# RWKV scan in an RWKV / DeltaNet / Mamba trunk: the chunk inverse applied to the scan's operands in batches, ahead of the scan

## The chip, the cores and the metric

The kernel runs on one core of a Trainium2 chip. The metric is the device time of one execution in microseconds; the time shown of the kernel before is the median of three executions. One more execution was profiled, and all rows below come from that one.

## What is computed

One residual layer over 16 learned meta tokens and 1024 frames of width 1024: a normalised input goes through one wide projection, then through three groups of heads (gated DeltaNet, RWKV-7, Mamba-2), and their outputs through one output projection. The change touches RWKV-7 alone: 8 heads of 64, each with a 64x64 state that is updated frame by frame.

```python
def rwkv7_recurrence(r, w, k, v, a, b):
    """S_t = S_{t-1} diag(w_t) + (S_{t-1} a_t) b_t^T + v_t k_t^T,  y_t = S_t r_t."""
    def step(state, inp):
        r_t, w_t, k_t, v_t, a_t, b_t = inp
        sa = jnp.einsum("bhvk,bhk->bhv", state, a_t)
        state = (state * w_t[:, :, None, :] + sa[..., None] * b_t[:, :, None, :]
                 + v_t[..., None] * k_t[:, :, None, :])
        return state, jnp.einsum("bhvk,bhk->bhv", state, r_t)
    ...
# in rwkv7_group: a = -kk, b = kk * a, with kk the l2-normalised keys
```

## The kernel before, in words

The kernel is a list of units: six of DeltaNet (`unit_a`, one head of 128 each), four of RWKV (`unit_b`, two heads of 64 each), two of Mamba (`unit_c`), and at the end the output stage (`unit_o`). Each unit is a Python generator. Its first part is projections: `proj` multiplies a 128-column weight tile with all frames, in pieces of some 350 columns, eight steps of the contraction and three float32r products a step; these are the matmuls `pj`. They are dense work of TensorE (PE) that waits for little. Its second part is the unit's own algebra, many short steps on PE, ScalarE (ACT) and VectorE (DVE), each of which hands over with a `yield`.

`schedule` (L1193) decides the order. It keeps an estimate of PE's clock, takes a unit's next short step when it believes its inputs to be ready, and fills PE with single projection matmuls until then. The units' order is the constant `PLAN`; some projections are put into a queue by `later` and are due at a given time. What the generators issue is then placed on each engine by the tile framework's scheduler, so the order of instructions on an engine is fixed before the run, and PE executes its list in order. `Meter` (L97) records every operation of the short steps, so most rows have the line L97 and are told apart by the tiles' names.

Short steps take their PSUM tiles through `ps` (L119): a unit has a lane, and a lane has two PSUM tiles in turn (`GB`), so a third one waits until the first has been read.

`unit_b` (L641) works on 17 chunks of 64 frames, the first one mostly padding. For each chunk it builds, for two heads at a time on the two halves of the 128 partitions: `ar` (the decayed a and r), `bk` (the decayed b and k), their masked products `gms` from the matmuls `bgr` (L97), and `bt`, the transposes of `bk` (matmuls `bbT`, ACT copies `bbt`). The lower triangular system of a chunk is inverted ahead of the scan, in blocks of 32: diagonal blocks by `solve32` on DVE, the block below by the 32x32 matmuls `bm1`, `bm2` (L796 to L806). The inverse stands in `gms[0]`, called `gb` in the scan; `gk` is the product with the keys, `v1_` the values.

The scan (L813 to L861) goes through the chunks one by one, three steps a chunk with a `yield` between them. Step one fills the PSUM tile `bsi`: `gk·v + ar·st`, and the output's first two terms beside it; ACT copies the first half to `b_x` (L830). Step two multiplies `b_x` by the inverse into the PSUM tile `bu` (L832) and starts the state update with `b_k·v`; DVE scales by `ib` into `u_`, a part of the tile `buv`. Step three adds `b_k·u`, makes the new state `sn` (tile `b_s`) on DVE, and adds `gb·u` to the output in `bsi`, which ACT copies to `by` (L852). Every one of these products is two matmuls of 64x64, one for each half of the array (`both`).

Of the kernel before, what the change touches and what calls it, by code (L numbers as in the profile page):

```python
# [19 lines left out]
MUL, ADD, SUB, MAX = ALU.mult, ALU.add, ALU.subtract, ALU.max  # L20
# [43 lines left out]
def bc(ap, axis, n):  # L64

    ap = ap.unsqueeze(axis)
    shape = list(ap.shape)
    shape[axis] = n
    return ap.broadcast_to(tuple(shape))
# [32 lines left out]
class Trunk:  # L102
# [538 lines left out]
    def unit_b(self, p):  # L641
        nc, sm = self.nc, self.sm
        v, act, pe, pool, sync = self.engines
        ident = self.ident
        yield 1, "proj"
        k, r = (self.one([128, 17, 64], f"b{x}{p}") for x in "kr")
# [4 lines left out]
        at_c = lambda t, c: t[c // 9][:, c % 9]  # L651
# [14 lines left out]
        for i, (out, bias) in enumerate(((e1[:, :, 1:], self.w0), (at, self.a0))):  # L666
            for s, e in ((0, 8), (8, 16), (16, 17)):
                ps = self.ps(f"bw{p}_{i}{s}")
# [5 lines left out]
        for s in range(0, 17, 3):  # L674
            e = min(s + 3, 17)
# [10 lines left out]
        ar, bk = ([self.one([128, 9 - i, 128], f"b{x}{p}_{i}") for i in range(2)] for x in ("ar", "bk"))  # L686

        ib = sm.tile([128, 17], F32, tag="b_ib", name="b_ib")
        hs = (slice(0, 64), slice(64, 128))
# [3 lines left out]
        ps = self.ps(f"bn{p}")  # L693
# [21 lines left out]
        gms = [[self.one([128, 9 - i, 128], f"bgm{p}_{x}{i}") for i in range(2)] for x in range(2)]  # L715
        banks = ((1, 5), (5, 9), (9, 13), (13, 17), (0, 1))
        for s, e in banks:
            pair = [self.ps(f"bgr{p}_{x}{s}") for x in range(2)]
            for c in range(s, e):
                for x in range(2):  # L720
                    for h in range(2):
                        pe.matmul(pair[x][hs[h], 128 * (c - s): 128 * (c - s) + 128], at_c(bk, c)[hs[h], hs[x]], at_c(ar, c)[hs[h]],
                                  start=True, stop=True)
# [9 lines left out]
        for s, e in banks:  # L733
            ps = self.ps(f"bbT{p}_{s}")
# [29 lines left out]
        uv = [self.one([128, 9 - i, 128], f"buv{p}_{i}") for i in range(2)]  # L764
        for s, e in ((0, 1), (1, 9), (9, 17)):
            ps = self.ps(f"bvT{p}_{s}")
            n, m = (e - s + 1) // 2, min(e - s, 2)
            for j in range(n):
                pe.transpose(ps[: 64 * m, 128 * j: 128 * j + 128], v_[:, 64 * (s + 2 * j): 64 * (s + 2 * j + m)], ident)
            for j in range(m):  # L770
                for h in range(2):
                    x = s % 9 + j
# [4 lines left out]
        for w in range(2):  # L777
            ps = self.ps(f"bbon{p}{w}")
# [14 lines left out]
        for i, (c0, c1) in enumerate(split):  # L793
            n = c1 - c0
# [15 lines left out]
        yield 12  # L810


        yt = self.one([128, 8, 128], f"by{p}")  # L813
        st, to_a, to_r = None, hs[0], hs[1]
        for c in range(17):
            gb, gk, a_r, b_k, uvc = (at_c(t, c) for t in (gms[0], gms[1], ar, bt, uv))
            u_, v1_ = uvc[:, 0:64], uvc[:, 64:]

            def both(out, cols, lhs, part, rhs, start, stop):
                for h in range(2):  # L820
                    pe.matmul(out[hs[h], cols], lhs[hs[h], part], rhs[hs[h]], start=start, stop=stop, skip_group_check=True)

            pq = self.ps(f"bsi{p}_{c}")
            both(pq, hs[0], gk, to_a, v1_, True, c == 0)
            if c:
                both(pq, hs[0], a_r, to_a, st, False, True)
                both(pq, hs[1], gk, to_r, v1_, True, False)
                both(pq, hs[1], a_r, to_r, st, False, False)
            x = self.tmp("b_x")
            act.copy(x[:, 0:64], pq[:, 0:64])  # L830
            yield
            pu = self.ps(f"bu{p}_{c}")  # L832
            both(pu, hs[0], gb, to_a, x[:, 0:64], True, True)
            if c < 16:
                pd = pu[:, 64:128]
                both(pu, hs[1], b_k, hs[1], v1_, True, False)
            v.tensor_scalar(u_, pu[:, 0:64], ib[:, c: c + 1], None, MUL)
            yield
            if c < 16:
                both(pu, hs[1], b_k, hs[0], u_, False, True)  # L840
                sn = self.tmp("b_s")
                w_ = wc[:, c + 1: c + 2]
                if c:
                    nc.scalar.activation(sn[:, 64:128], st, AF.Copy, scale=w_)
                    v.scalar_tensor_tensor(sn[:, 0:64], pd, w_, sn[:, 64:128], MUL, ADD)
                else:
                    v.tensor_scalar(sn[:, 0:64], pd, w_, None, MUL)
                sn = sn[:, 0:64]
            if c:
                both(pq, hs[1], gb, to_r, u_, False, True)  # L850
                for h in range(2):
                    nc.scalar.copy(yt[hs[(c - 1) % 2], (c - 1) // 2, hs[h]], pq[hs[h], 64:128])  # L852
                self.lag = max(0.2, self.lag - 0.21)
            if c < 16:
                st = sn
            if c == GATE:
                yield 8
                g = self.one([128, 17, 64], f"bg{p}")
                gated = self.later(36 + p, self.shifted(36 + p, 12 + p, g, gate=True), DUES[4])
                g = flat(g)  # L860
            else:  # L861
                yield
# [16 lines left out]
        for w in range(2):  # L879
            ps = self.ps(f"byT{p}_{w}")  # L880
# [518 lines left out]
```

## Time and profile before

| | |
|---|---|
| Median of three executions | 1450.17 us (1448.45 to 1453.15) |
| The profiled execution's own time | 1442.35 us |
| Span from its first to its last instruction | 1440.4 us |
| Mean granted TensorE clock | 0.985 |
| Instructions | 28351 |
| PE / weight loads / DVE / ACT / GpSimd (POOL) busy | 96% / 83% / 65% / 50% / 12% |

How to read it: a matmul's record begins when it enters the array; matmuls are pipelined and their ends are modelled, so a duration is longer than the time a matmul adds to a row of them. That time is the distance from one start to the next. A float32 matmul leaves two records and two weight loads, a float32r one and a transpose leave one of each. The size written before a shape, such as 64\*64 or 128\*128, is the part of the array that the matmul uses.

### The profile page before, as it was taken

What the parts mean: (1) busy time and instruction counts of PE and PEld (TensorE: products, weight loads), DVE (VectorE), ACT (ScalarE), POOL (GpSimd) and SP (SyncE); (2) the same over time, 40 slices, a digit from 0 to 9 for tenths busy, and PEclk for the clock granted to TensorE, in tenths of its full rate; (3) what the DMA queues carried; (4) which work ended last, traced back from release to release, by engine and by line L of the source; (5) the groups of instructions that cost most, each with busy time, mean ns of one, the idle gap of its engine ahead of it and who ended that gap; (6) DMA issues with size and microseconds to landing.
All of it is one profiled execution on the core that took longest, in us unless ns stands there. A gap on an engine that the chain in (4) does not pass through costs nothing.

```text
span 1440.4 us, 28351 instructions
## 1 busy us (share of the span) xinstructions
PE 1389.7 (96%) x10801; PEld 1188.8 (83%) x10801; DVE 935.4 (65%) x2610; ACT 719.9 (50%) x2020; POOL 172.4 (12%) x223
## 2 busy tenths in 40 slices
PE   4999999999999999999999999999999999899997
PEld 4999888778788789979778898889998987677786
DVE  6548586467667348879625788655589876632663
ACT  6365445446364464545636655444666355632520
POOL 2111010000010011111001110001231110201000
PEclk9999999999999999999979999999999999999999
DMA  7354243213234143234422242234553322743861
GB/s 233 78 131 87 56 102 71 57 40 88 44 66 112 30 133 89 57 82 89 100 60 60 54 108 62 59 88 89 133 124 77 71 38 56 233 133 101 254 198 44
DMA packets 120458, 136.43 MB, mean 95 GB/s; under 512 B 39867, under 2 KB 72379, under 8 KB 120323
## 3 DMA queue, kind: packets, MB, share of 16 engines
q1 hardware_dynamic: 102755, 102.64, 24.1%
q0 software_dynamic: 17568, 31.99, 13.4%
q8 instruction: 85, 1.39, 0.4%
q14 instruction: 50, 0.41, 0.1%
HBM read 116.99 MB, written 17.60 MB: 93 GB/s over the span
## 4 chain that ended last, share of the span: by engine, by line
PE 78%; issue 6%; ACT 6%; DMA 4%; DVE 4%; POOL 0%; SPq 0%; DVEq 0%; ACTq 0%; POOLq 0%
PE pj L97 45%; PE po L97 5%; PE bsi L97 4%; PE bu L97 3%; PE bgr L97 3%; PE am L97 2%; PE aops L97 1%; PE cdg L97 1%; ACT bbt L97 1%; DMA or<-in_w_out_dram 1%; PE ads L97 1%; PE av L97 1%; DMA omrw<-d_mix 1%; PE aks L97 1%; PE agk L97 1%
## 5 line engine op out<-in xcount | busy, mean ns | idle before, releaser
L97 PE MATMUL pj<-hh,w 128*128 128x350 f32 (+7 forms) x2736 | 757.6, 348 | 0.2 <-ACT hh L264 0.2
L97 PEld LDWEIGHTS pj<-hh,w 128*128 128x128 f32 x2736 | 483.4, 190 | 25.7 <-issue 4.4
L97 PE MATMUL pj<-hl,w 128*128 128x350 f32 (+7 forms) x1368 | 474.8, 347 | 0.0
L97 PEld LDWEIGHTS pj<-hl,w 128*128 128x128 f32 x1368 | 260.2, 190 | 11.8 <-issue 1.2
L153 POOL DMA_DIRECT2D w<-in_wt_dram x122 | 106.5, 873 | 878.6 <-ACT w L151 600.5
L151 ACT ACTIVATE w<-wr 128x512 fp32r<-128x512 f32 x122 | 76.8, 630 | 72.7 <-PE pj L97 70.7
L97 PE MATMUL po<-ow,omw 128*128 128x512 f32 x408 | 97.7, 400 | 4.0 <-ACT omw L1088 3.2
L97 PEld LDWEIGHTS po<-ow,omw 128*128 128x128 f32 x408 | 77.5, 191 | 24.2 <-ACT omw L1088 3.6
L97 PE MATMUL po<-ow,ome 128*128 128x512 f32 x360 | 90.5, 402 | 2.1 <-ACT ome L1088 1.6
L97 PEld LDWEIGHTS po<-ow,ome 128*128 128x128 f32 x360 | 66.6, 189 | 17.7 <-ACT ome L1088 2.2
L152 ACT CAST w<-wr 128x512 fp32r<-128x512 f32 x122 | 74.4, 609 | 0.1
L97 DVE TENSOR_SCALAR buv<-bu,b_ib 128x64 f32<-128x64 f32 x68 | 19.2, 282 | 71.6 <-PE bu L97 71.5
L97 PE MATMUL bsi<-buv,bgm 64*64 64x64 f32 x784 | 63.0, 230 | 0.7 <-DVE b_s L97 0.2
L97 DVE TENSOR_TENSOR s_tmp<-alb 33x30 f32<-33x30 f32 (+9 forms) x180 | 57.0, 317 | 3.2 <-DMA alb<-d_l 1.9
L97 DVE TENSOR_TENSOR alb<-alb,s_tmp 33x30 f32<-33x30 f32 (+9 forms) x180 | 57.0, 317 | 3.0 <-POOL alb L97 1.6
L97 PEld LDWEIGHTS bsi<-buv,bgm 64*64 64x64 f32 x784 | 43.5, 136 | 16.5 <-issue 4.6
L184 DVE SCALAR_TENSOR_TENSOR cbc<-pj,pack,cbc 128x346 f32<-128x346 f32 (+4 forms) x72 | 41.1, 571 | 20.5 <-ACT cbc L181 19.7
L852 ACT COPY by<-bsi 64x64 f32<-64x64 f32 x128 | 26.5, 207 | 48.9 <-PE bsi L97 47.6
L1089 DVE TENSOR_TENSOR ome<-omre,ome 128x512 fp32r<-128x512 f32 (+2 forms) x40 | 22.5, 600 | 36.2 <-ACT ome L1088 36.1
L97 PE MATMUL bgr<-bar,bbk 64*64 64x128 f32 x544 | 45.4, 277 | 0.0
L97 PE MATMUL bu<-buv,bbt 64*64 64x64 f32 x512 | 42.4, 234 | 0.0
L184 DVE SCALAR_TENSOR_TENSOR cx<-pj,pack,cx 128x346 f32<-128x346 f32 (+2 forms) x54 | 31.1, 576 | 16.9 <-ACT cx L181 15.9
(324 smaller groups left out, 2390.3 us busy)
## 6 DMA issues: line engine op xcount, KB each, us to landing
wr<-in_wt_dram SPq DMA_DIRECT2D x122, 256.0 KB, 3.4
w<-in_wt_dram POOLq DMA_DIRECT2D x122, 256.0 KB, 4.8
or<-in_w_out_dram SPq DMA_DIRECT2D x32, 256.0 KB, 3.8
omrw<-d_mix SPq DMA_DIRECT2D x32, 256.0 KB, 3.9
clt<-d_cs SPq DMA_DIRECT2D x24, 256.0 KB, 4.9
omre<-d_mix SPq DMA_DIRECT2D x24, 256.0 KB, 2.8
btw<-d_tw SPq DMA_DIRECT2D x8, 544.0 KB, 5.9
x<-in_x_dram SPq DMA_DIRECT2D x8, 512.0 KB, 7.7
```

What stands on the lines that cost most here:

```text
L97: return op(out, *args, **kw)
L151: nc.scalar.activation(w[:, 1], raw, AF.Copy, scale=-1.0)
L152: nc.scalar.copy(w[:, 0], raw)
L153: nc.gpsimd.dma_start(w[:, 1], src, accum_op=ADD)
L184: nc.vector.scalar_tensor_tensor(acc[:, a + z: b], p[:, o + z - s: o + b - a - s], cw[:, 3 - s: 4 - s], acc[:, a + z: b], MUL, ADD)
L852: nc.scalar.copy(yt[hs[(c - 1) % 2], (c - 1) // 2, hs[h]], pq[hs[h], 64:128])
L1089: nc.vector.tensor_tensor(t[:, 1], raw, t[:, 0].bitcast(F32), SUB)
```

## The change

The scan loses its step in the middle. Its system `u = ib · gb · (gk·v + ar·st)` is linear in the state, so the two products with the inverse `gb` that don't need the state are made ahead of the scan, for eight chunks at a time (the first chunk alone): `bta` is `gb` on `ar` (with `ar`'s a-half transposed first: transposes `baT`, ACT copies into a part of `uv`), `bkv` is `gk·v`, copied by ACT into a new tile `kv`, and `btk` is `gb` on `kv`, scaled by `ib` on DVE into `uv`. In the scan, step one is now `ar·st` with one DVE operation that scales and adds what lies in `uv`; step two is the state update and the output's last term. The copy `b_x` and the PSUM tile's first half of `bu` are gone, and `bu` is 64 columns wide. A unit's scan has 192 matmuls of 64x64 where it had 260; the batches add 100 of them and 16 transposes a unit. In all PE has 8378 matmuls, transposes among them, where it had 8186.

```diff
+        to_a, to_r = hs
+        kv = self.one([128, 17, 64], f"bkv{p}")
+        for s, e in ((0, 1), (1, 9), (9, 17)):
+            i, x, n = s // 9, s % 9, e - s
+            if s:
+                for k in (0, 4):
+                    ps = self.ps(f"baT{p}_{s}{k}")
+                    for j in range(4):
+                        pe.transpose(ps[0:64, 128 * j: 128 * j + 128], ar[i][:, x + k + j, 0:64], ident)
+                    for h in range(2):
+                        act.copy(uv[i][hs[h], x + k: x + k + 4, 0:64], ps[0:64].rearrange("p (c t) -> p c t", c=4)[:, :, hs[h]])
+            ps = self.ps(f"bkv{p}_{s}")
+            for c in range(s, e):
+                both(ps, in8(c - s), at_c(gms[1], c), to_a, at_c(uv, c)[:, 64:], True, True)
+            act.copy(kv[:, s:e], as8(ps, n))
+            yield
+            if s:
+                ps = self.ps(f"bta{p}_{s}")
+                for c in range(s, e):
+                    both(ps, in8(c - s), at_c(uv, c), to_a, at_c(gms[0], c)[:, 0:64], True, True)
+                act.copy(ar[i][:, x: x + n, 0:64], as8(ps, n))
+            ps = self.ps(f"btk{p}_{s}")
+            for c in range(s, e):
+                both(ps, in8(c - s), at_c(gms[0], c), to_a, kv[:, c], True, True)
+            v.tensor_tensor(uv[i][:, x: x + n, 0:64], as8(ps, n), bc(ib[:, s:e], 2, 64), MUL)
+            yield 0.1
...
-            pq = self.ps(f"bsi{p}_{c}")
-            both(pq, hs[0], gk, to_a, v1_, True, c == 0)
             if c:
-                both(pq, hs[0], a_r, to_a, st, False, True)
+                pq = self.ps(f"bsi{p}_{c}")
+                both(pq, hs[0], a_r, to_a, st, True, True)
                 both(pq, hs[1], gk, to_r, v1_, True, False)
                 both(pq, hs[1], a_r, to_r, st, False, False)
-            x = self.tmp("b_x")
-            act.copy(x[:, 0:64], pq[:, 0:64])
-            yield
-            pu = self.ps(f"bu{p}_{c}")
-            both(pu, hs[0], gb, to_a, x[:, 0:64], True, True)
+                v.scalar_tensor_tensor(u_, pq[:, 0:64], ib[:, c: c + 1], u_, MUL, ADD)
+                yield
             if c < 16:
-                pd = pu[:, 64:128]
-                both(pu, hs[1], b_k, hs[1], v1_, True, False)
-            v.tensor_scalar(u_, pu[:, 0:64], ib[:, c: c + 1], None, MUL)
-            yield
-            if c < 16:
-                both(pu, hs[1], b_k, hs[0], u_, False, True)
+                pd = self.ps(f"bu{p}_{c}")[:, 0:64]
+                both(pd, hs[0], b_k, hs[1], v1_, True, False)
+                both(pd, hs[0], b_k, hs[0], u_, False, True)
```

The change moves PE's instructions, too, since the order is planned anew. The first place is one chunk of the scan of the third RWKV unit (chunk 3). Before, on PE:

```order
L97 MATMUL bsi_3_5499<-buv_0_5134,bgm_10_4349 64x64 x2
L97 MATMUL bsi_3_5499<-b_s,bar_0_4072 64x64 x2
L97 MATMUL bsi_3_5499<-buv_0_5134,bgm_10_4349 64x64 x2
L97 MATMUL bsi_3_5499<-b_s,bar_0_4072 64x64 x2
L97 MATMUL pj_2_5456<-hh,w_0_5165 128x350
L97 MATMUL pj_2_5456<-hl,w_0_5165 128x350
L97 MATMUL bu_3_5515<-b_x,bgm_00_4347 64x64 x2
L97 MATMUL bu_3_5515<-buv_0_5134,bbt_0_4523 64x64 x2
L97 MATMUL pj_2_5456<-hh,w_0_5165 128x350 x2
L97 MATMUL pj_2_5456<-hl,w_0_5165 128x350
L97 MATMUL pj_2_5456<-hh,w_0_5165 128x350
L97 MATMUL bu_3_5515<-buv_0_5134,bbt_0_4523 64x64 x2
```

The same chunk on PE with the change:

```order
L97 MATMUL bsi_3_5743<-b_s,bar_0_4076 64x64 x2
L97 MATMUL bsi_3_5743<-buv_0_5214,bgm_10_4495 64x64 x2
L97 MATMUL bsi_3_5743<-b_s,bar_0_4076 64x64 x2
L97 MATMUL bu_3_5774<-buv_0_5214,bbt_0_4647 64x64 x2
L97 MATMUL pj_2_5535<-hh,w_1_5251 128x350 x2
L97 MATMUL bu_3_5774<-buv_0_5214,bbt_0_4647 64x64 x2
L97 MATMUL bsi_3_5743<-buv_0_5214,bgm_00_4493 64x64 x2
L97 MATMUL pj_2_5535<-hl,w_1_5251 128x350
L97 MATMUL pj_2_5535<-hh,w_1_5251 128x350
```

A chunk has two groups of 64x64 matmuls between projections where it had three, and the projections that stood between the first two of them are gone from here.

The second place is the batch of chunks 1 to 8 of the same unit, on PE with the change, ahead of its scan; before, nothing stood here:

```order
L97 MATMUL baT_10_5480<-pack,bar_0_4076 64x128 x4
L97 MATMUL baT_14_5487<-pack,bar_0_4076 64x128 x4
L97 MATMUL pj_1_5463<-hh,w_1_5251 128x350 x2
L97 MATMUL bkv_1_5494<-buv_0_5214,bgm_10_4495 64x64 x9
L97 MATMUL bta_1_5540<-bgm_00_4493,buv_0_5214 64x64
L97 MATMUL bkv_1_5494<-buv_0_5214,bgm_10_4495 64x64
...
L97 MATMUL bta_1_5540<-bgm_00_4493,buv_0_5214 64x64 x9
L97 MATMUL pj_1_5463<-hl,w_1_5251 128x350
L97 MATMUL btk_1_5558<-bkv_5465,bgm_00_4493 64x64 x7
L97 MATMUL baT_90_5577<-pack,bar_1_4077 64x128 x4
L97 MATMUL btk_1_5558<-bkv_5465,bgm_00_4493 64x64 x9
```

The scheduler has laid the end of `bkv` and the beginning of `bta` one by one beside each other, and one or two projections stand between the groups.

The third place is the same batch of the fourth unit, on PE with the change. It falls beside the block inverse of the DeltaNet unit a1 (`am`) and the beginning of a1's scan (`av`, `ads`, `aks`):

```order
L97 MATMUL baT_14_8553<-pack,bar_0_6959 64x128 x2
L97 MATMUL bkv_1_8560<-buv_0_8253,bgm_10_7217 64x64 x5
L97 MATMUL am_8172<-add_8089,alo_7046 64x64 x8
L97 MATMUL bkv_1_8560<-buv_0_8253,bgm_10_7217 64x64 x11
L97 MATMUL pj_1_8365<-hl,w_0_8225 128x512
L97 MATMUL am_8190<-alo_7046,add_8089 64x64 x8
L97 MATMUL av_0_8210<-avt_7779,alo_7046 16x128
L97 MATMUL bta_1_8616<-bgm_00_7215,buv_0_8253 64x64 x11
L97 MATMUL ads_0_8219<-a_vn,akd_7067 128x128
L97 MATMUL bta_1_8616<-bgm_00_7215,buv_0_8253 64x64 x5
L97 MATMUL btk_1_8634<-bkv_8526,bgm_00_7215 64x64 x3
L97 MATMUL aks_1_8241<-a_s,ak_6748 128x128
```

Before, the first chunks of this unit's scan stood beside the same work of a1; now the batches do, and the scan begins later.

## Rows read from the trace of the kernel before

**Rows 1.** The page: busy us, share of the span, instructions; then tenths in 40 slices.

```profile
PE 1389.7 (96%) x10801; PEld 1188.8 (83%) x10801; DVE 935.4 (65%) x2610; ACT 719.9 (50%) x2020; POOL 172.4 (12%) x223
PE   4999999999999999999999999999999999899997
```

**Rows 2.** The page: chain that ended last, shares by line.

```profile
PE pj L97 45%; PE po L97 5%; PE bsi L97 4%; PE bu L97 3%; PE bgr L97 3%; PE am L97 2%; PE aops L97 1%; PE cdg L97 1%; ACT bbt L97 1%; DMA or<-in_w_out_dram 1%; PE ads L97 1%; PE av L97 1%; DMA omrw<-d_mix 1%; PE aks L97 1%; PE agk L97 1%
```

**Rows 3.** Waits, 236 to 820 us: who waited for whom, us in total, times, longest.

```profile
PEld bu L97 <- ACT b_x L97: 8.2, 31, 0.9
PEld bbT L97 <- ACT bbt L97: 3.0, 5, 0.8
PE bbT L97 <- ACT bbt L97: 1.0, 4, 0.4
PE bu L97 <- ACT b_x L97: 1.0, 2, 0.7
```

**Rows 4.** Windows: stretch, its length, busy us (and instructions) by engine, granted clock, DMA.

```profile
236.00:820.00 584.00, 575.65 (x5492) 478.01 (x5492) 372.86 (x1018) 298.78 (x907) 64.19 (x85) 0.97 0.31 72
```

**Rows 5.** Timeline of PE: start us, us until the last end, instructions; projections alone.

```profile
256.20 0.32 PE L97 MATMUL pj<-hl,w 128*128 128x348 f32 x1
256.36 0.48 PE L97 MATMUL pj<-hh,w 128*128 128x348 f32 x2
```

**Rows 6.** Timeline of PE: scan matmuls one after the other, halves alternating.

```profile
263.25 0.28 PE L97 MATMUL bsi<-b_s,bar 64*64 64x64 f32 x4
263.36 0.28 PE L97 MATMUL bsi<-buv,bgm 64*64 64x64 f32 x4
263.48 0.28 PE L97 MATMUL bsi<-b_s,bar 64*64 64x64 f32 x4
```

**Rows 7.** Timeline of PE: a burst of the scan among projections.

```profile
472.03 0.58 PE L97 MATMUL pj<-hh,w 128*128 128x350 f32 x2
472.45 0.32 PE L97 MATMUL pj<-hl,w 128*128 128x350 f32 x1
472.70 0.33 PE L97 MATMUL bu<-buv,bbt 64*64 64x64 f32 x4
472.86 0.28 PE L97 MATMUL bsi<-buv,bgm 64*64 64x64 f32 x4
473.08 0.58 PE L97 MATMUL pj<-hh,w 128*128 128x350 f32 x2
```

**Rows 8.** Timeline of PE: eight transposes and what follows.

```profile
163.51 1.03 PE L97 MATMUL bbT<-pack,bbk 128*128 128x128 f32 x8
164.30 0.40 PE L97 MATMUL pj<-hh,w 128*128 128x336 f32 x1
```

**Rows 9.** Timeline of PE: eight matmuls on one half, and what follows.

```profile
174.54 1.14 PE L97 MATMUL am<-add,alo 64*64 64x64 f32 x16
175.61 0.44 PE L97 MATMUL pj<-hl,w 128*128 128x386 f32 x1
```

**Rows 10.** Groups, and durations min/median/max in ns, of the copies and products beside PE.

```profile
L97 ACT COPY bbt<-bbT x80: 205/367/372, 164.4 to 643.8; 64x256 f32<-64x256 f32 x64, 64x64 f32<-64x64 f32 x16
L152 ACT CAST w<-wr 128x512 fp32r<-128x512 f32 x50 | 30.6, 612 | 0.1
L97 DVE TENSOR_TENSOR bgm<-bgr,pack x40: 282/681/693, 149.2 to 631.6; 128x512 f32<-128x512 f32 x32, 128x128 f32<-128x128 f32 x8
```

**Rows 11.** Windows at half clock, all engines (the column before the last two is the clock).

```profile
239.00:245.80 6.80, 6.80 (x31) 5.61 (x31) 4.00 (x6) 1.31 (x3) 0.00 (x0) 0.50 0.01 2
467.70:471.10 3.40, 3.40 (x23) 2.82 (x23) 1.51 (x4) 0.00 (x0) 0.00 (x0) 0.50 0.02 5
723.70:740.80 17.10, 17.10 (x103) 12.30 (x104) 1.93 (x7) 4.89 (x15) 0.86 (x1) 0.50 0.17 32
```

**Rows 12.** Windows, of the projections' instructions alone (no POOL column).

```profile
714.00:723.70 9.70, 1.90 (x7) 0.69 (x5) 0.00 (x0) 0.00 (x0) 1.00 0.41 164
723.70:740.80 17.10, 7.07 (x11) 2.67 (x11) 0.00 (x0) 0.00 (x0) 0.50 0.17 32
```

More of the change, by code (lines that the diff above doesn't have):

```diff
@@ L810, in unit_b, with both @@
         yield 12
+        def both(out, cols, lhs, part, rhs, start, stop):
+            for h in range(2):
+                pe.matmul(out[hs[h], cols], lhs[hs[h], part], rhs[hs[h]], start=start, stop=stop, skip_group_check=True)
+        to_a, to_r = hs
+        in8 = lambda c: slice(64 * c, 64 * c + 64)
+        as8 = lambda ps, n: ps[:, : 64 * n].rearrange("p (c t) -> p c t", c=n)
+        kv = self.one([128, 17, 64], f"bkv{p}")
[6 more added lines that the diff above has]
+                        pe.transpose(ps[0:64, 128 * j: 128 * j + 128], ar[i][:, x + k + j, 0:64], ident)
+                    for h in range(2):
+                        act.copy(uv[i][hs[h], x + k: x + k + 4, 0:64], ps[0:64].rearrange("p (c t) -> p c t", c=4)[:, :, hs[h]])
[14 more added lines that the diff above has]
+            yield 0.1
         yt = self.one([128, 8, 128], f"by{p}")
-        st, to_a, to_r = None, hs[0], hs[1]
+        st = None
         for c in range(17):
@@ L817, in unit_b @@
             u_, v1_ = uvc[:, 0:64], uvc[:, 64:]
-            def both(out, cols, lhs, part, rhs, start, stop):
-                for h in range(2):
-                    pe.matmul(out[hs[h], cols], lhs[hs[h], part], rhs[hs[h]], start=start, stop=stop, skip_group_check=True)
-            pq = self.ps(f"bsi{p}_{c}")
-            both(pq, hs[0], gk, to_a, v1_, True, c == 0)
             if c:
-                both(pq, hs[0], a_r, to_a, st, False, True)
+                pq = self.ps(f"bsi{p}_{c}")
+                both(pq, hs[0], a_r, to_a, st, True, True)
                 both(pq, hs[1], gk, to_r, v1_, True, False)
                 both(pq, hs[1], a_r, to_r, st, False, False)
-            x = self.tmp("b_x")
-            act.copy(x[:, 0:64], pq[:, 0:64])
-            yield
-            pu = self.ps(f"bu{p}_{c}")
-            both(pu, hs[0], gb, to_a, x[:, 0:64], True, True)
-            if c < 16:
-                pd = pu[:, 64:128]
-                both(pu, hs[1], b_k, hs[1], v1_, True, False)
-            v.tensor_scalar(u_, pu[:, 0:64], ib[:, c: c + 1], None, MUL)
-            yield
-            if c < 16:
-                both(pu, hs[1], b_k, hs[0], u_, False, True)
+                v.scalar_tensor_tensor(u_, pq[:, 0:64], ib[:, c: c + 1], u_, MUL, ADD)
+                yield
+            if c < 16:
+                pd = self.ps(f"bu{p}_{c}")[:, 0:64]
+                both(pd, hs[0], b_k, hs[1], v1_, True, False)
+                both(pd, hs[0], b_k, hs[0], u_, False, True)
                 sn = self.tmp("b_s")
```

## The prediction

> **What bounds the kernel now.** I read the page first: its busy shares and its strip of 40 slices. TensorE (PE) is busy 96% of the span and stands at 8 or 9 tenths of it, from the second slice to the last but one; VectorE (DVE) has 65%, ScalarE (ACT) 50% [rows 1]. Busy shares of PE come from modelled ends, so I checked them against the chain that ended last: the projections alone (`pj`) are 45% of it; the scan of the RWKV units shows as `bsi` 4% and `bu` 3% [rows 2]. Then I asked what PE waits for. From 236 to 820 us, the stretch that holds the four RWKV scans, it stood idle 1.0 us for the copy `b_x` between the steps of a chunk [rows 3]: the scan is a long chain, but other work stands between its links. In that stretch PE is busy 575.65 of 584 us [rows 4]. So the price of this change is what it makes PE issue and how often PE changes between tile sizes, not the length of the chain.
>
> The timeline of PE gives those prices, start to start. Projection matmuls follow each other every 0.16 us [rows 5]. Matmuls of 64x64 whose two halves of the array alternate take 0.115 us for two (four records, since a float32 matmul has two), so 0.0575 each [rows 6]. Where a burst of these stands among projections, the rows from 472.03 to 473.08 us hold three projections (0.48) and four small matmuls (0.23) and yet last 1.05 us [rows 7]: **a round trip to the 64x64 tiles and back costs 0.34 us**. Part of it comes late: the first two projections behind the burst and the next stand 0.42 us apart, not 0.32. If that part has another cause, 0.20 us is left, and I keep this as the lower price.
>
> **The change, part by part.** It touches unit_b alone. In the printed order PE's matmuls are the same up to about 236 us and, from about 966 us of the old trace on, the same to the end; the output stage is untouched.
>
> (a) Small matmuls. Each unit's scan loses 34 of `bsi` and 34 of `bu`, 272 in four units; the batches `bkv`, `bta`, `btk` add 34, 32 and 34 a unit, 400 in all. Net 128 more, x 0.0575 = **+7.4 us**.
>
> (b) Transposes. `baT` adds 64. Eight `bbT` transposes took 0.79 us from the first to what follows [rows 8], 0.10 each: **+6.3 us**.
>
> (c) Tile sizes. Scan steps have two bursts a chunk where they had three, but the batches bring bursts of their own, some of them transposes among 32x32 or 64x64 work. I counted, in both printed orders, the places where PE's next matmul has another tile size: 744 before, 664 now. That is 40 round trips less, x 0.34 = **-13.6 us**; with the lower price -8.0.
>
> (d) Same half. In the batches the scheduler lays one matmul of `bkv` beside one of `bta`, and the alternation of halves is lost: successive 64x64 matmuls on the same tile rise from 125 to 255. Eight matmuls that all use one half took 1.07 us to the next projection [rows 9]; less 0.1 for leaving, that is 0.12 each, 0.063 above the alternating price. 130 x 0.063 = 8.2 at most; nothing, if neighbours further on overlap all the same. I take +5, nearer the row, because its form is the same: **+5 us**.
>
> (e) Waits inside the batches. Every batch is one PSUM tile that ACT or DVE empties before the next but one can be written, since a lane has two. The nearest stage is `bbT` and its copies `bbt`: 15 such banks in the stretch cost PE 1.0 us by its own row and 3.0 us by its weight loads [rows 3], 0.07 to 0.2 us a bank. The batches have 11 tiles a unit, 44 in all: +2.9 to +8.8 us. I take **+5 us**; the projections put between are only one to three, and unit 3 has fewer still.
>
> (f) The copy `b_x` goes: 68 copies and the wait behind them. PE's own row gives 1.0 us, its weight loads 8.2 us [rows 3]. Part of that wait lies under the change of tile size that (c) counts, so I take **-4 us**.
>
> (g) ACT and DVE. ACT loses 68 copies of 64 columns, 0.21 us each if they cost what the shortest `bbt` copies do (14 us), and gets 32 copies of 64x256 at 0.37, 16 of 128x512 at 0.61 and 4 short ones: some 22 us, net +8. DVE keeps one operation of 64 columns a chunk and gets eight of 512 columns at 0.68: net +5 or 6 [rows 10]. Both have room in the stretch (ACT 299 of 584 us, DVE 373) [rows 4], so I cost this at nothing; without that room it shows as longer waits in (e), whose upper end covers it. POOL's and SP's queues get no new DMA.
>
> (h) Clock. Three times beside the RWKV scans the granted clock is 0.50, so 1.2 and not 2.4 GHz: for 6.8, 3.4 and 17.1 us [rows 11]. Ahead of the long one, PE did 32x32 and 64x64 work with 7 projections in 9.7 us; in it, 11 in 17.1 [rows 12]. These 27.3 us lie where the new batches go; at half clock they cost up to 13.7 us. They could go or double: in the new order the work just ahead of each stays as it was, and small tiles follow it as before. I take **0**, with -13.7 and +13.7 as the ends.
>
> Sum: 7.4 + 6.3 - 13.6 + 5 + 5 - 4 = **+6.1 us**. The profiled execution took 1442.35 us and would take 1448.5; it lies 7.8 us under the median 1450.17 of the three timed runs, so the forecast for a median is **1456.3 us**, slower by 0.4%. A measurement of this kernel can tell about 0.3%, 4.4 us, from no change.
>
> A page speaks to the reading of the first paragraph. The Trainium skill (Perfetto Trace Analysis, Identifying the Most-Contended Engine) says that busy matmul time is a poor measure of how near TensorE is to its limit, and asks for the busy share of weight loads. Here that share is 83% [rows 1], so by the rule there would be room for the additions. The trace agrees in the share and not in the room: PE's own idle time in the stretch is 8.35 us [rows 4].
>
> **The rivals.**
>
> *The clock stays up (faster).* The place is unit 3's scan, 723.7 to 740.8 us. If the batches finish the inverse ahead and the scan's shorter bursts let projections stand closer, the clock never falls there, and in units 0 and 2 neither: -13.7 on top of +6.1 is -7.6, **1442.6 us**. It decides as soon as more than 10.5 us of that loss go, since then the sum is under -4.4. For it: the scan's matmuls fall from 260 to 192 a unit. Against: the new order has, in just that place, batches among 32x32 work and the scan of a1 with one projection in 34 rows of the order. Chance 0.13.
>
> *The additions fit into PE's slack (faster).* The terms (a), (b), (d) and (e) then cost nothing, since PE has gaps, and (c) and (f) stand: -17.6, **1432.6 us**. For it: weight loads idle 17% of the span [rows 1]. Against: in the stretch PE itself idles 8.35 us of 584 [rows 4], less than the additions need. Chance 0.07. This is what the rule of the page above would make of the time.
>
> *The clock falls in the batches (slower).* A unit's batches are 100 small matmuls and 16 transposes, 5.75 + 1.6 = 7.4 us at full clock, with few projections between; at half clock each unit pays 7.4 more. Two units give +14.8 on top of +6.1, **1471 us**; four give +29.4, 1486. For it: the longest fall came behind small-tile work [rows 11, 12]. Against: `bgr`, as long a run of 64x64 tiles, stands in four units and has not always brought it down. Chance 0.10. The Trainium skill (TensorE: Matmul & The Clock Gate, Part 4) says that transposes do not count as TensorE being busy in the way matmuls do, by which `baT` would favour this case. No row here separates transposes from the work around them.
>
> *It cancels out (no change).* The round trips saved pay for the matmuls and the chain's own waits for those of the batches: about **1450 us**. That is the sum with (d) at nothing and (f) at its upper end. Chance 0.12.
>
> **How the numbers follow.** The forecast, PE pays for the added work, has 0.58. Its own range: the lower ends of (d), (e), (c at 0.34) and the full (f) give 7.4 + 6.3 - 13.6 + 0 + 2.9 - 8.2 = -5.2; the upper, with (c) at -8.0, 8.2, 8.8 and -1.0, gives +21.7: 1445 to 1472. Within it I put 0.40 over +4.4 us and 0.18 within. Slower: 0.40 + 0.10 = 0.50. Within 0.3%: 0.18 + 0.12 + 0.01 (a clock that stays up in part) = 0.31. Faster: 0.12 + 0.07 = 0.19. The range of 8 in 10 leaves out most of the slack case and the worst of the clock: **1440 to 1474 us**.
>
> **What would show it.** Right: PE's busy time rises by some 5 us in the stretch and nothing moves after it; `baT` near 0.10 us each; the three batches at 0.06 to 0.09 us a matmul; fewer returns of `pj` behind bursts; `b_x` gone from ACT and its place among the waits of PE taken by the copies for `bkv` and `btk`. Wrong: the half-clock stretches of units 0, 2 and 3 gone or several times longer; the projections themselves spaced more closely over the stretch, which would mean that a round trip costs more than 0.34 us; or a part behind 966 us that differs, though its order is the same.

## The result and the profile after

The changed kernel took a median of **1455.0 us** (1444.04 to 1464.06, 15 runs) beside 1446.92 us (1442.17 to 1462.96, 15 runs) for the kernel before: ratio **1.0061, 95% interval 1.0043 to 1.0079**, by that ratio some 8.8 us slower. The forecast was +6.1 us. The profiled execution of the changed kernel took 1452.12 us, span 1450.4 us, granted clock 0.986.

The page after, busy times, the strip of PE and that of its clock, and the chain by line (to be held against [rows 1, 2]):

```profile
PE 1390.2 (96%) x11121; PEld 1199.6 (83%) x11121; DVE 936.5 (65%) x2618; ACT 729.3 (50%) x2004; POOL 171.1 (12%) x223
PE   4999999999999999998999999999999999899997
PEclk9999999999999999999999999999999999999999
PE pj L97 41%; PE po L97 5%; PE bsi L97 3%; PE bgr L97 3%; PE am L97 2%; PE bu L97 2%; DMA or<-in_w_out_dram 1%; PE aops L97 1%; PE cdg L97 1%; PE ads L97 1%; DMA x<-in_x_dram 1%; DMA omrw<-d_mix 1%; ACT bbt L97 1%; PE agk L97 1%; PE av L97
```

PE has 320 matmul records more and is busy 0.5 us longer in all; the projections have fallen from 45% to 41% of the chain. PE's order is the same up to 236 us, and again from the projection that began at 966.0 us before and begins at 971.8 us now. So the windows of these two stretches compare like with like (length, then busy us and instructions of PE, PEld, DVE, ACT, POOL, clock, DMA share, GB/s). Before:

```profile
236.00:966.00 730.00, 721.12 (x6554) 608.63 (x6554) 482.66 (x1358) 373.52 (x1120) 80.56 (x106) 0.98 0.32 73
```

After:

```profile
236.00:971.80 735.80, 719.59 (x6874) 618.31 (x6874) 482.94 (x1366) 384.09 (x1104) 78.97 (x106) 0.99 0.32 73
```

The stretch is 5.8 us longer, and PE isn't busier in it: its busy time fell by 1.5 us and its idle time rose from 8.9 to 16.2 us. A stall explains more of this result than work does. The waits of 236 to 826 us after show which (who waited for whom, us, times, longest):

```profile
PEld bu L97 <- DVE buv L97: 6.1, 29, 0.2
PEld bsi L97 <- DVE b_s L97: 5.9, 27, 0.3
PE czT L97 <- DVE ctmp L97: 5.3, 1, 5.3
PE bm L97 <- DVE bdd L790: 3.1, 2, 2.5
PEld bkv L97 <- ACT buv L97: 0.9, 3, 0.4
PEld btk L97 <- ACT bkv L97: 0.3, 2, 0.2
```

The same two waits of the weight loads in the scan, for `buv` and `b_s`, in the kernel before (236 to 820 us):

```profile
PEld bu L97 <- DVE buv L97: 4.0, 19, 0.2
PEld bsi L97 <- DVE b_s L97: 3.3, 14, 0.4
```

The wait for `b_x` [rows 3] is gone, and the short waits for `buv` and `b_s`, which were there before, have grown from 7.3 to 12.0 us. The batches themselves hardly wait (0.9 and 0.3 us). But `czT`, a transpose of the Mamba unit c0 that the change doesn't touch, waits 5.3 us in one piece.

That wait can be followed back through four engines. PE's timeline first (start, us, what, idle before and releaser), after the change:

```profile
668.61 0.32 PE L97 MATMUL pj<-hl,w 128*128 128x350 f32 x1
674.20 0.90 PE L97 MATMUL czT<-pack,cz 128*128 128x128 f32 x3 [5.27 <-DVE ctmp L97]
```

Then DVE, where `ctmp` is queued behind the diagonal-block inverse of RWKV unit b3 (`blb`):

```profile
658.27 0.19 DVE L97 TENSOR_TENSOR s_tmp<-blb 68x30 f32<-68x30 f32 x1 [7.09 <-DMA blb<-d_l]
673.60 0.54 DVE L97 SCALAR_TENSOR_TENSOR ctmp<-ctmp,czT 128x384 f32<-128x384 f32 x1
```

Then SP's DMA queue:

```profile
638.10 4.37 SPq L747 DMA_DIRECT2D d_l<-bgm  x8
649.56 0.35 SPq L150 DMA_DIRECT2D wr<-in_wt_dram  x1
650.15 0.26 SPq L97 DMA_DIRECT2D blb<-d_l  x1
```

The view of SP's own waits (636 to 652 us) names what its weight load (L150) waited for, ACT's copy `w` (L152):

```profile
SPq L150 <- ACT w L152: 7.8, 2, 7.0
```

And ACT, whose `w` copy (`CAST`) gives that weight load its buffer:

```profile
640.91 0.59 ACT L999 COPY cz<-pj 128x512 f32<-128x512 f32 x1 [10.80 <-PE pj L97]
641.40 6.97 ACT L97 COPY bbt<-bbT 64x256 f32<-64x256 f32 x20
648.39 0.63 ACT L151 ACTIVATE w<-wr 128x512 fp32r<-128x512 f32 x1
648.93 0.60 ACT L152 CAST w<-wr 128x512 fp32r<-128x512 f32 x1
```

The blocks had been issued to `d_l` by 642.5 us, but their read-back `blb` stands on SP's queue behind a weight load that doesn't start before ACT frees its buffer at 649.5 us. In the kernel before the same two loads stand the other way round:

```profile
632.56 3.28 SPq L747 DMA_DIRECT2D d_l<-bgm  x7
637.24 0.26 SPq L97 DMA_DIRECT2D blb<-d_l  x1
645.23 2.00 SPq L150 DMA_DIRECT2D wr<-in_wt_dram  x2
```

There the read-back left first, and the weight load waited for ACT with nobody behind it. The new order had exchanged two neighbours on a queue to which the change adds nothing.

### The profile page after: what moved, and what is told of

It reads as the page before. It is cut to its first block, busy times and chain, and to the rows that moved or that the text cites. A ratio compares the mean times of both kernels' runs of the same rounds, so it can differ in the third digit from the quotient of the medians.

```text
span 1450.4 us, 29026 instructions
## 1 busy us (share of the span) xinstructions
PE 1390.2 (96%) x11121; PEld 1199.6 (83%) x11121; DVE 936.5 (65%) x2618; ACT 729.3 (50%) x2004; POOL 171.1 (12%) x223
## 3 DMA queue, kind: packets, MB, share of 16 engines
q0 software_dynamic: 17568, 31.99, 13.2%
## 4 chain that ended last, share of the span: by engine, by line
PE 75%; DMA 7%; DVE 6%; issue 6%; ACT 5%; POOL 1%; SPq 0%; DVEq 0%; ACTq 0%; POOLq 0%
PE pj L97 41%; PE po L97 5%; PE bsi L97 3%; PE bgr L97 3%; PE am L97 2%; PE bu L97 2%; DMA or<-in_w_out_dram 1%; PE aops L97 1%; PE cdg L97 1%; PE ads L97 1%; DMA x<-in_x_dram 1%; DMA omrw<-d_mix 1%; ACT bbt L97 1%; PE agk L97 1%; PE av L97 1%
## 5 line engine op out<-in xcount | busy, mean ns | idle before, releaser
L97 PE MATMUL pj<-hh,w 128*128 128x350 f32 (+7 forms) x2736 | 750.0, 347 | 0.2 <-ACT hh L264 0.2
L152 ACT CAST w<-wr 128x512 fp32r<-128x512 f32 x122 | 74.3, 609 | 0.0
L97 DVE TENSOR_TENSOR s_tmp<-blb 68x30 f32<-68x30 f32 (+14 forms) x120 | 38.7, 323 | 8.0 <-DMA blb<-d_l 7.1
L97 PE MATMUL bsi<-b_s,bar 64*64 64x64 f32 x512 | 41.4, 231 | 0.0
L97 DVE SCALAR_TENSOR_TENSOR buv<-bsi,b_ib,buv 128x64 f32<-128x64 f32 x64 | 18.0, 282 | 34.8 <-PE bsi L97 34.3
```

The source lines that it names most:

```text
L97: return op(out, *args, **kw)
L152: nc.scalar.copy(w[:, 0], raw)
```

## Experiments

To read them I split each profiled execution, from the starts of its matmuls. **Lost to clock** is half of the time that was run at half clock. **Stalls** are what a distance between two starts exceeds, by over 0.3 us, the median that the same pair of neighbours (tile, columns, type) has in all these traces (of a distance at half clock, half is taken). **Work** is the rest. Two profiles of the changed kernel differ by 2.5 us in work and 2.4 in stalls; smaller differences aren't read. **Even clock** is rougher and uses every timed execution: the median of span times granted clock, less the same median of the kernel before on that chip, good to some 2 us. It is an estimate, since it takes half of all time at half clock to be lost. Ratios, too, are to executions of the kernel before on the same chip.

| kernel | median us | ratio to before (95%) | work | stalls | lost to clock | even clock, us to before |
|---|---|---|---|---|---|---|
| before | | | 1364.3 | 36.0 | 20.5 | |
| after | 1455.0 | 1.0061 (1.0043 to 1.0079) | 1368.0 | 45.0 | 17.1 | |
| after, again | 1454.67 | 1.0050 (1.0021 to 1.0079) | 1365.5 | 42.6 | 25.6 | +11.0 |
| scan alone | 1431.75 | 0.9907 (0.9876 to 0.9938) | 1317.9 | 55.2 | 37.5 | -28.0 |
| batches added | 1498.71 | 1.0374 (1.0334 to 1.0414) | 1414.0 | 39.1 | 20.5 | +52.4 |
| spread, 128x128 | 1608.02 | 1.1129 (1.1095 to 1.1164) | 1420.1 | 43.8 | 117.8 | +61.7 |
| spread, 64x64 | 1475.36 | 1.0204 (1.0167 to 1.0242) | 1380.6 | 46.0 | 30.7 | +25.5 |
| load on GpSimd | 1458.73 | 1.0081 (1.0052 to 1.0110) | 1365.8 | 43.3 | 30.7 | +8.0 |
| loads exchanged | 1445.11 | 0.9963 (0.9935 to 0.9992) | 1366.4 | 40.2 | 15.4 | +4.6 |
| paired | 1449.24 | 1.0010 (0.9984 to 1.0037) | 1359.5 | 44.5 | 23.9 | +5.0 |
| paired, load on GpSimd | 1443.70 | 0.9974 (0.9948 to 0.9999) | 1360.0 | 45.1 | 15.4 | +3.2 |
| the same, again | 1443.99 | 0.9987 (0.9965 to 1.0009) | 1359.7 | 45.4 | 17.1 | +4.2 |
| paired, load on ACT | 1446.30 | 0.9990 (0.9962 to 1.0018) | 1360.6 | 45.7 | 11.9 | +5.8 |
| apart | 1469.73 | 1.0160 (1.0116 to 1.0204) | 1362.8 | 53.5 | 30.7 | +13.2 |

The theory at the outset: PE is full, so the time follows the work that PE issues, plus a price for each round trip to the small tiles, plus stalls that the new order happens to bring. Its rivals: the scan's chain bounds, the additions are hidden, or the clock decides.

### The two halves of the change, each by itself

```diff
@@ scan alone: the whole block of batches is replaced by
+        for i, (s, e) in enumerate(split):
+            pool.memset(uv[i][:, :, 0:64], 0.0)
+        yield
```

> The kernel after with the batches taken out (no transposes of a, no three groups of products, no copies of theirs; GpSimd sets the starting values of u to zero instead), so the terms of gb times a, gk times v and gb times their product are left out of the result and only the shorter scan is run. Theory (TensorE is full, so time follows the work it issues): in the two traces the scan's bsi and bu products take 31.8 us less of TensorE after the change, so this kernel stands about 32 us below the kernel before, 1415 us where before is 1447 (ratio 0.978, 0.973 to 0.983). Rival 1 (the scans' length was what bounded, and the batches are hidden): about the time of the kernel after, 1450 to 1456. Rival 2 (each scan's first-to-last time, shorter by 23 to 38 us, is gained in full): 100 us or more below before.

```diff
@@ batches added: the batches stand ahead of the old scan; bta goes where the scan overwrites it
-                act.copy(ar[i][:, x: x + n, 0:64], as8(ps, n))
+                act.copy(uv[i][:, x: x + n, 0:64], as8(ps, n))
```

> The kernel before, unchanged in its scan, with all of the batches run ahead of it; their last result is written into the place that the scan overwrites and is not used. Theory (TensorE is full): the batches take 41.1 us of TensorE in the trace after, so this one stands 41 us above the kernel before, 1488 us where before is 1447 (ratio 1.028, range 1.022 to 1.034), and with the run of the scan alone the two differences sum to what the change gave, +9 us within 6. Rival 1 (the additions fit in what TensorE has free): at most 10 us above before. Rival 2 (the change cost what it cost by stalls that its new order brought, not by its work): the two differences don't sum; they leave out 5 us or more.

In time both missed: -14 us where -32 was expected, +53 where +41 was. Nor do the two sum to the +9 that was expected of them: they leave +39, and +24 at even clock. In work they fit each other and the change: -46.4 and +49.7 sum to +3.3, where the change made +3.7. The batches take 41.5 us of the second one's work, as expected; some 8 us more lie outside them, with 848 changes of tile size where there were 744. What the first didn't give back shows on its own window from 236 to 900 us:

```profile
236.00:900.00 664.00, 633.58 (x5695) 548.09 (x5689) 452.02 (x1269) 339.55 (x986) 78.92 (x106) 0.96 0.33 75
```

and on its longest wait of PE:

```profile
PE pj L97 <- DVE cbc L187: 9.0, 1, 9.0
```

PE idles 30.4 of 664 us, and the clock is down. Of the idle time the view of waits puts 18.6 us down to VectorE and 10.7 to ScalarE: in the new order, with 46 us less of work on PE, they don't keep it fed. Of the gain, 19 us go to stalls and 17 to the clock. So "time follows PE's work" holds for what is added, and only in part for what is taken away. The scans became shorter (with the change unit b2's lasts 38 us where it lasted 61, unit b3's 64 where it lasted 98), and no gain of that size shows in the changed kernel or in the scan alone: the chain of the scan didn't bound.

The batches cost 53 us although weight loads were busy only 83% of the span before. That is against the reading of the Trainium skill (Perfetto Trace Analysis, Identifying the Most-Contended Engine) by which there was room; PE's own idle time told more. The rule also asks for the share of peak flops, which wasn't worked out here.

### The price of a round trip between tile sizes

```diff
@@ behind each chunk of each batch but the last: 128x128
+                if c < e - 1:
+                    nc.tensor.matmul(ps[:, 64 * (c + 1 - s): 64 * (c + 1 - s) + 8], ident, ident[:, 0:8], start=True, stop=True)
@@ control: 64x64
+                if c < e - 1:
+                    nc.tensor.matmul(ps[0:64, 64 * (c + 1 - s): 64 * (c + 1 - s) + 8], ident[0:64, 0:64], ident[0:64, 0:8], start=True, stop=True)
```

> The kernel after with a 128x128 matmul of 8 columns, whose result is overwritten, behind each chunk of each batch but the last (168 of them): each takes the array out of its 64x64 tiles and back, 957 changes of tile size where there were 664, 146 round trips more. Theory (0.34 us for a round trip, as priced in the prediction): 50 us for the trips and 168 times 0.06 = 10 us for the matmuls, +60 us over the kernel after, about 1515 (ratio to before 1.047). Rival 1 (the low price of the prediction, 0.20 us): 29 + 10 = +39 us, about 1494 (1.033). Rival 2 (a change of tile size costs nothing by itself, and the gaps seen round the bursts are waits on other engines): as with small matmuls in their place, +10 to +20 us, 1465 to 1475.

> The control to the run with 128x128 matmuls: the same 168 matmuls of 8 columns at the same places, but 64x64 on the first half of the array, so that the tile size doesn't change (655 changes; 442 successive pairs on one half in place of 275). Theory: 168 times 0.06 us = +10 us over the kernel after, about 1465 (ratio to before 1.012), and if two in a row on one half cost 0.12 us each, as the prediction's high end has it, +20 us, 1475 (1.019). The difference between the two runs divided by 151 is the price of a round trip less that of a same-half pair.

The work differs by 39.5 us over 151 round trips: **0.26 us each**, between the two prices of the prediction, 0.34 and 0.20, and not nothing. The stretches at full clock alone agree: from a 64x64 matmul of the batches to the short one and back the median distances are 149 and 186 ns, in the control 32 and 58, which is 0.245 us less. The control's own matmuls cost 12.6 / 168 = 0.075 us each, 0.09 by the second profile of the changed kernel, though 167 more of them follow another on the same half: less than 0.12. In time the control came out where the expectation has the dear case, 1.0204 beside 1.019; but at even clock it is 14.5 us above the changed kernel, 0.086 for each matmul, and the rest is clock.

The time of the first one is another matter: 93 us over what the theory had. At even clock it is 51 us above the changed kernel, where 60 was expected. The strips of the granted clock, first the 128x128 kernel:

```profile
PEclk9999997699599859999996599999999999999999
```

and its longest stretch at half clock:

```profile
551.40:599.20 47.80, 47.80 (x325) 39.13 (x321) 2.52 (x6) 5.54 (x13) 0.00 (x0) 0.50 0.00 1
```

The strip of its control:

```profile
PEclk9999998999799999999999999999999999999999
```

Among batches whose small matmuls were pulled apart by short 128x128 ones, the clock fell to 1.2 GHz and stayed there for up to 47.8 us, with no idle time between PE's records. This is the rival "the clock falls in the batches" at full strength, brought about by the added matmuls. The control isn't free of it: 23.9 us at half clock from 366 us on, which begin in the batches of unit b1. Nor is the changed kernel itself. In its first profile only 3.4 us of the batches (at 239 us) ran at half clock; in its second it was 6.8 us at 244 us and 13.7 us in the batches of unit b3:

```profile
735.70:749.40 13.70, 13.70 (x146) 10.91 (x143) 0.64 (x2) 4.91 (x13) 0.00 (x0) 0.50 0.01 3
```

### The two loads on SP's queue

First the read-back of b3 was given to GpSimd's queue.

```diff
-        sync.dma_start(lb[0:68], d1)
+        (nc.gpsimd if p == 3 else nc.sync).dma_start(lb[0:68], d1)
+        self.lag += DMA
```

> The kernel after with one load moved: unit b3's read-back of the diagonal blocks (blb from d_l) is issued by GpSimd's queue and no longer behind the weight load on SyncE's, which waits for ScalarE. Theory (TensorE is full, so a stall that the new order of work brought is paid): the 7.1 us that VectorE waits for this load go, and with them the 5.3 us that TensorE waits for ctmp at 674 us; 5 us below the kernel after, less 1 or 2 for a new order behind it: ratio to before 1.0025 (1.001 to 1.005) where the kernel after has 1.006. Rival (such a stall is made up later, since other work only moves): no difference from the kernel after, 1.006.

It did not do what it was for. GpSimd's queue also carries weights:

```profile
653.84 0.88 POOL L153 DMA_DIRECT2D w<-in_wt_dram  x1 [10.60 <-PE pj L97]
654.71 0.59 POOL L753 DMA_DIRECT2D blb<-d_l  x1
```

The load went out no earlier, VectorE still waited 6.3 us for it and `czT` 4.3 us. It tests nothing but the choice of queue. So the other load was moved, the one in front:

```diff
-            nc.sync.dma_start(raw, src)
+            (nc.scalar if (i, h) == (1, 1) else nc.sync).dma_start(raw, src)
```

> The kernel after with one weight load (wr1_1, the one that stands ahead of unit b3's read-back blb on SyncE's queue) issued by ScalarE, right behind the copy that releases its buffer. SyncE then issues blb as soon as the writes of d_l are through, as in the kernel before; TensorE's order is the same up to the place where it waited for ctmp. Theory (TensorE is full and a stray stall is paid): VectorE's wait of 7.1 us for blb falls under 1 us, TensorE's wait of 5.3 us for ctmp goes, and the time is 4 to 6 us below the kernel after: ratio to before 1.002 (1.000 to 1.004). Rival 1 (the wait comes back elsewhere, since the order behind is planned anew): both waits go and the time is that of the kernel after, 1.005 to 1.006. Rival 2 (the load was late for another reason): VectorE still waits over 5 us.

SP's queue in this kernel:

```profile
638.84 4.37 SPq L747 DMA_DIRECT2D d_l<-bgm  x8
644.87 0.26 SPq L97 DMA_DIRECT2D blb<-d_l  x1
```

PE's timeline at the same place:

```profile
669.52 0.33 PE L97 MATMUL pj<-hh,w 128*128 128x350 f32 x1
669.68 0.49 PE L97 MATMUL czT<-pack,cz 128*128 128x128 f32 x3
```

Both waits are gone, and PE goes from the projection to `czT` without a gap. The time is 0.9963 of before, under the range that was expected (1.000 to 1.004): 12 to 14 us below the changed kernel by the ratios, more than twice the 5.3 us of the stall. Part of the rest stands right behind the stall. The window there, changed kernel (stall, then the half clock):

```profile
668.60:674.20 5.60, 0.33 (x4) 0.04 (x2) 5.60 (x21) 0.74 (x2) 0.00 (x0) 0.86 0.08 24
672.70:679.50 6.80, 5.30 (x19) 5.30 (x20) 6.48 (x17) 2.43 (x5) 0.86 (x1) 0.50 0.23 38
```

and with the loads exchanged:

```profile
669.60:676.40 6.80, 6.80 (x46) 6.78 (x45) 5.74 (x16) 4.18 (x11) 1.62 (x4) 1.00 0.48 93
```

Where PE had stood idle, the clock fell to 1.2 GHz for 6.8 us; where it hadn't, the clock stayed up. In the profiles, PE's order matched piece by piece, this kernel leads by 5.3 us just behind `czT`, 7.2 us a little later, 10.4 us at 722 us and 8.0 at the end. Over all executions, the two kernels stand 4.6 and 11.0 us above the kernel before at even clock. So some 6.4 us of the gap are the stall and the order behind it; the rest is clock (median granted clock 0.9865 against 0.983), and I can't take it apart further.

The same figures say what the lead over the kernel before is: 5.4 us in time and none at even clock, where this kernel is still 4.6 us behind (95% interval 2 to 7). Its granted clock is higher (median 0.9865 against 0.980 on that chip), and it is the clock that wins.

### Cheaper transposes

```diff
-                for k in (0, 4):
-                    ps = self.ps(f"baT{p}_{s}{k}")
-                    for j in range(4):
-                        pe.transpose(ps[0:64, 128 * j: 128 * j + 128], ar[i][:, x + k + j, 0:64], ident)
+                pool.tensor_copy(kv[:, s:e], ar[i][:, x: x + n, 0:64])
+                ps = self.ps(f"baT{p}_{s}")
+                for j in range(4):
+                    pe.transpose(ps[:, 128 * j: 128 * j + 128], flat(kv[:, s + 2 * j: s + 2 * j + 2]), ident)
... (the copies out of `ps` follow the new layout)
```

> The kernel after with the transposes of a made for two chunks at once: GpSimd first packs eight chunks of a side by side, and 8 transposes of 128x128 for a unit take the place of 16 of 128x64 (32 in place of 64 in all; 623 changes of tile size in place of 664). Theory (time follows TensorE's work): 32 times 0.11 = 3.5 us and 20 round trips by 0.34 = 7 us less, together 10 us below the kernel after if no new stall comes: ratio to before 0.999 (0.996 to 1.003). Rival 1 (transposes lie in gaps, changes of tile size are cheap): no difference from the kernel after, 1.006. Rival 2 (the packing on GpSimd is a new link at the head of the batches, and the new order of work brings its own stalls): as the kernel after or slower, 1.006 to 1.012.

Work fell by 8.5 us against the first profile of the changed kernel and 6.0 against the second (`baT` from 8.2 to 4.3 us), the ratio to 1.001: as the theory had it. With the load on GpSimd's queue as well, twice:

> Both: the paired transposes and unit b3's load on GpSimd's queue. Theory: the two gains add where both stalls were there; if the paired kernel has lost the wait for ctmp already, this is as the paired kernel alone, 0.999, else 0.995. Rival (both worthless): 1.006.

> The paired kernel with the load on GpSimd's queue once more, since its interval only just left 1 out. Theory (10 us less of TensorE's work than the kernel after, stalls alike): 8 to 12 us below the kernel after, ratio to before 0.997 to 1.001. Rival (the gain of the first runs was a clock that happened to stay up): as the paired kernel alone, 1.001, with a granted clock no higher than that of before.

About 11 us below the changed kernel on one chip (1443.99 beside 1454.67); against the kernel before one interval just leaves out 1 and the other doesn't, so a gain over before isn't shown, and at even clock both are 3 to 4 us behind it. What the load added to the paired kernel is mostly clock (median 0.986 against 0.983): VectorE still waits 5.5 and 5.0 us for the load, and the wait of `czT` falls only from 2.6 us to 1.9 and 1.5. On ScalarE's queue:

> The paired kernel with unit b3's load issued on ScalarE's queue in place of GpSimd's, where it stands between the scaled and the plain copy of a weight. Theory (any queue that also carries weights makes the load wait for the same released weight buffer): VectorE still waits 5 to 7 us for the load, and the time is that of the paired kernel, 0.997 to 1.001. Rival (SyncE's queue alone was the cause): the wait goes, and 3 to 5 us more are won, 0.994 to 0.997.

VectorE waited 7.0 us, the time is the paired kernel's: each of the three queues tried carries weights, and on each the load was held up. Of the versions that do the whole change, only the one with the loads exchanged beats the kernel before in every series with its interval clear of 1, and it does so by the clock.

### Keeping the halves alternating

```diff
-            for c in range(s, e):
-                both(ps, in8(c - s), at_c(gms[1], c), to_a, at_c(uv, c)[:, 64:], True, True)
-            act.copy(kv[:, s:e], as8(ps, n))
+            with self.tc.high_priority(100):
+                for c in range(s, e):
+                    both(ps, in8(c - s), at_c(gms[1], c), to_a, at_c(uv, c)[:, 64:], True, True)
+                act.copy(kv[:, s:e], as8(ps, n))
```

> The kernel after with the first group of products and its copy given a higher priority, so that it is not mixed with the third group of the batch before: successive products on the same half of the array fall from 275 to 243, changes of tile size from 664 to 656. Theory (two in a row on one half cost almost nothing, changes of tile size 0.34 us a round trip): 1 to 3 us below the kernel after, ratio 1.004 to 1.006, apart from stalls of the new order. Rival (a same-half pair costs 0.06 us or more): 2 us more.

Missed by both: work is 5.2 us down, but the new order waits 4.9 us for `ctmp`, 4.9 us for `cbc` and 5.5 us for `bdd`, and the time is 1.6% over before. A priority meant for one group rearranged the rest.

### The changed kernel once more

> The kernel after once more, beside the two paired kernels on one chip. Theory: 9 us over the kernel before (ratio 1.006), of it 10 at an even clock. Rival (the difference between chips is as large as that between these kernels): under 1.003.

1.0050, with `czT` again waiting 5.3 us and 6.8 us at half clock beside it (from 674.3 us): the stall is in both profiled executions, not an accident of one. In time it is 6.1 us above the kernel before, where 9 was expected; at even clock 11.0, where 10 was. The interval doesn't leave out the rival's 1.003.

## Why the prediction was right

The bound was right, and so was the size of the work: PE is full and pays. Without the exchange of the two loads the change costs 4.6 us at even clock, where the sum of (a) to (f) was +6.1. But the change as it is costs 11.0 us at even clock (some 10 in the first series, where the kernel before has no clock on record, if it is there what it is on the other chips). That its time came out near the forecast is in part luck: a stall that no term had costs some 6 us, and a clock that (h) put at nothing gives back 2 to 5.

- **(a) to (d), the work, forecast +5.1 us: +3.7 by the first profile, +1.2 by the second.** The bursts of unit b2 show the prices, PE's timeline after:

```profile
473.49 1.04 PE L97 MATMUL baT<-pack,bar 128*64 128x128 f32 x8
474.28 0.56 PE L97 MATMUL pj<-hh,w 128*128 128x350 f32 x2
474.92 0.79 PE L97 MATMUL bkv<-buv,bgm 64*64 64x64 f32 x18
475.69 0.27 PE L97 MATMUL bta<-bgm,buv 64*64 64x64 f32 x1
...
476.55 0.75 PE L97 MATMUL bta<-bgm,buv 64*64 64x64 f32 x18
477.23 0.42 PE L97 MATMUL pj<-hl,w 128*128 128x350 f32 x1
```

  (The dots stand for the piece in which `bkv` and `bta` lie one by one.) Eight `baT` take 0.79 us, 0.10 each, as priced. `bkv` takes 0.77 us for nine, `bta` 0.68 for nine: 0.086 and 0.076, within 0.06 to 0.09. In the piece between, 475.69 to 476.55 us, where `bkv` and `bta` lie one by one on the same half, 14 matmuls take 0.86 us, 0.061 each. So (d) was mis-sized: near nothing, not +5. Why the eight `am` of [rows 9] took 0.12 each is open. The round trip of (c) was mis-sized, too: 0.26 us, not 0.34, so -10.4 and not -13.6. (Its lower price of 0.20 is a slip: the rows give 0.34 - 0.10 = 0.24.) The two errors nearly cancel.
- **(e) and (f), waits, forecast +5 and -4: +9 of stalls by the first profile, +6.6 by the second (+7.3 us of idle time in the stretch).** This is the step that failed. The waits inside the batches are 1.2 us in the rows shown and 2.1 in all rows that name a releaser, not 5 (and the batches have 12 tiles a unit, not 11). What (f) gave can't be told apart: the wait for `b_x` is gone, those for `buv` and `b_s` have grown by 4.7 us. I priced waits only where the change puts instructions, and (g) said of SP's queue that it gets no new DMA. True, but the order on it changed: two loads were exchanged, PE stood still for 5.3 us, and exchanging them back took 6.4 of the 11.0 us at even clock away.
- **(h), the clock, forecast 0: -3.4 us in the first profile, +5.1 in the second.** Over all executions the clock gave back some 5 us in the second series (11.0 at even clock, 6.1 in time) and some 2 in the first. In the first profile the 17.1 us at half clock in unit b3's scan [rows 11] are gone, as the first rival had it, though its saving didn't come whole: the stall brought 6.8 us at half clock of its own. In the second, 13.7 us at half clock stand in b3's batches, as the rival "the clock falls in the batches" had it for one unit. With the stall away the median granted clock is 0.9865 against 0.980 for before on that chip, and it gives back 10 us (4.6 behind at even clock, 5.4 ahead in time). So the rival "the clock stays up" holds for the change without its stall, and in part for the change as it is.
- **Nothing moves after 966 us:** the order doesn't, yet the difference grows from 5.8 to 9.3 us. One half-clock stretch (1369 us) is in this execution and not in that of before; the rest I can't name.
- **PE busy 5 us longer in the stretch:** wrong, it fell by 1.5 us. Busy time counts a matmul longer at half clock, and this execution had 20.4 us of half clock in the stretch where the one before had 30.7.
- **The rule of the Trainium skill on transposes** (TensorE: Matmul & The Clock Gate, Part 4), named beside the rival on the batches: the paired kernel has 32 of the change's transposes where it had 64, and the same median clock, 0.983; no run here shows an effect.

## What to carry to other kernels

When a planner sets the order, compare every queue's order before and after, DMA queues included: a load that has slipped behind one that waits for a buffer can cost more than the change itself. On an engine that is full, price added work by its starts and count the round trips between tile sizes, but don't expect removed work back in full, since the other engines may not keep up. Judge a variant by work, stalls and clock apart, or an order that happens to suit the clock is taken for a better kernel: with the loads exchanged the change looks 0.4% faster than before, and at even clock it is 0.3% slower.

## What was not expected of the hardware

A 5.3 us gap on PE went with 6.8 us at half clock that began in it, and closing the gap removed both; a gap of 4.3 to 5.3 us at the same `czT` has 6.8 us at half clock beside it in five more profiles (the changed kernel again, the load on GpSimd's queue, both spread ones, "apart"). And PE was busy for all of 47.8 us that it ran at half clock, mostly on 64x64 matmuls and 128x128 matmuls of 8 columns in turn; with 64x64 matmuls in place of the latter, 30.7 us were lost to the clock in the whole execution, not 117.8. Half clock on a busy PE doesn't need the 128x128 ones, though: in the second profile of the changed kernel it lasted 13.7 us on the batches of unit b3 and the small work of a1.
